# A two-layer trunk on one core: seven block products at the end of the first stage, and a setup for the S5 mixer spread over other engines and another stage

## The chip, the cores and the metric

The kernel runs on one core of one Trainium2 chip. The metric is the device time of one execution in microseconds (us). Engines are named as in the profile: PE is TensorE's matmul side and PEld its weight load, DVE is VectorE, ACT is ScalarE, POOL is GpSimd, SP is SyncE. A name with a q at its end (ACTq, POOLq, SPq) is that engine's instruction that issues a DMA.

## The reference

Two layers over x of 512 positions by 1024 columns, all in float32. The first has an SSD (Mamba-2) mixer, the second an S5 mixer, and each has a SwiGLU block before and after it.

```python
D_MODEL, SEQ, DEPTH, FFN_DIM = 1024, 512, 2, 2816

def swiglu(h, w_in, w_out):
    gate, up = jnp.split(h @ w_in, 2, axis=-1)
    return (jax.nn.silu(gate) * up) @ w_out

def reference(x, ...):
    for i in range(DEPTH):
        x = x + 0.5 * swiglu(rmsnorm(x, ffn1_norm[i]), ffn1_w_in[i], ffn1_w_out[i])
        h = rmsnorm(x, mix_norm[i])
        x = x + (ssd_mixer(h, ...) if i % 3 == 0 else s5_mixer(h, ...))
        x = x + 0.5 * swiglu(rmsnorm(x, ffn2_norm[i]), ffn2_w_in[i], ffn2_w_out[i])
    return rmsnorm(x, final_norm)

def s5_mixer(h, ...):                      # 64 groups of 16 columns, 64 complex states each
    lam_bar = jnp.exp(lam * step)
    b_bar = ((lam_bar - 1.0) / lam)[..., None] * lax.complex(b_re, b_im)
    # states[t] = lam_bar * states[t-1] + b_bar @ u[t];  y[t] = Re(c @ states[t]) + d * u[t]
    # then gelu, a product with glu_w, and value * sigmoid(gate)
```

What depends on the S5 weights alone (powers of lam_bar, the operators built from b, c and d, and tables of cosines and sines of its angles) can be made before the S5 mixer's input is there.

## The kernel before

Six stages follow each other: `f1_0` (SwiGLU), `ssd`, `f2_0` (SwiGLU), `f1_1` (SwiGLU), `s5`, `f2_1` (SwiGLU). In the profiled execution they end at about 390, 807, 1148, 1496, 1630 and 1981 us.

The residual stream is kept transposed as eight tiles `xT[d]` of 128 columns by 512 positions. Every float32 operand of a matmul is split into a high and a low part, and a product takes three matmuls (high by high, low by high, high by low). For weights, ACT casts the high part `whi` from the loaded `wst`, and DVE subtracts to get `wlo`. For a stage's normed input the parts are `H[d]` and `L[d]` (`hH`, `hL` in the profile).

**A SwiGLU stage** (`ffn`) has 22 pairs: a pair is one block of 128 gate columns and the block of 128 up columns beside it. They come in three parts, `PARTS` = (0, 8), (8, 15), (15, 22). After each part come eight out-projection columns d = 0..7: the part's activations `ah`, `al` times one block of out-weights, added to `xT[d]` by DVE.

- A *plain* pair is 2 x 8 x 3 = 48 matmuls with 512 columns (lines 374 to 376).
- A pair *as seven products* uses a block scheme over 2 x 2 blocks with seven block products instead of eight: 7 x 4 x 3 = 84 matmuls with 256 columns (line 445). It needs sums of input blocks, the forms (`forms`: tiles `hx`, `h1`, each again high by ACT and low by DVE), sums of weight blocks (`wx`, `wst`, made partly by DMAs that accumulate, issued on POOL), and more DVE work behind each product.

In `f1_0` all 22 pairs are plain. In `f2_0` the first three (`PLAIN`) are plain and 19 are as seven products; in `f1_1` and `f2_1` all 22.

**Order.** The tile framework's scheduler sets the order of instructions on each engine by its own estimate. Within `manual_schedule(engines=MAN)` (`f2_0` and all later stages) PE keeps the order in which the code is written; the other engines are ordered by the scheduler except for instructions that are pinned. In `f1_0` the scheduler orders PE too. Whatever the origin, the order on each engine is fixed when the program is built: an instruction that waits holds up all behind it on that engine.

**Work for S5 in other stages.** A list `fill` of closures is passed to `ffn`, and `pop()` runs the next one after each pair and each column: 22 + 24 = 46 pops, of which the columns are pops 8 to 15, 23 to 30 and 38 to 45. In `f1_0` this list holds the S5 setup: `lam` (lam_bar, its powers `PR`, `PI`, the angles), `ops(i)` for i = 0..15 (operators of four groups each: six DVE products and sums of 512 or 576 elements, line 1064, tiles `p_Ht`, `p_G`, `p_t`), `ops_pe(i)` (transposes and small products on PE; ACT copies the result into `p_ks`, DVE adds the diagonal with d by 64 small instructions in all, line 1349, and eight DMAs on ACT's queue write it out, line 1353), and `tables(i)` for i = 0..7 (`p_cs`, `p_tb`, from the angle powers `p_UC`, `p_US` by doubling, for eight of the 64 groups each, written to `d_t` by POOL).

**The step from `f2_0` to `f1_1`.** Behind the last columns of `f2_0` DVE adds `xT[6]` and `xT[7]` (line 683), makes `hL` of column 6 and 7 (lines 272, 286), the forms `hx` (lines 303, 307), the low parts of the first pair's weights (line 410) and the norm `nw_*` (lines 147 to 156), while PE goes on with products of the first pair of `f1_1` as far as their operands are there.

## Time and profile before

| what | value |
|---|---|
| median of 3 runs | 1981.26 us (1981.21 to 1982.32) |
| profiled execution: its own time | 1983.18 us |
| profiled execution: span | 1981.4 us, so 1.8 us lie outside the span |
| PE busy in the span | 1964.9 us (99%) |
| DVE busy | 1524.8 us (77%) |
| ACT busy | 944.7 us (48%) |
| POOL busy | 237.1 us (12%) |
| granted TensorE clock | 0.999 |

The profile is one execution. A busy share is an average over the six stages, and the engines' loads differ between the stages. PE takes its matmuls strictly in order, so whether a stage is bound by PE or by what feeds it is seen from PE's idle time in that stage and from what ended it.

### The profile page before, as it was taken

What the parts mean: (1) busy time and instruction counts of PE and PEld (TensorE: products, weight loads), DVE (VectorE), ACT (ScalarE), POOL (GpSimd) and SP (SyncE); (2) the same over time, 40 slices, a digit from 0 to 9 for tenths busy, and PEclk for the clock granted to TensorE, in tenths of its full rate; (3) what the DMA queues carried; (4) which work ended last, traced back from release to release, by engine and by line L of the source; (5) the groups of instructions that cost most, each with busy time, mean ns of one, the idle gap of its engine ahead of it and who ended that gap; (6) DMA issues with size and microseconds to landing.
All of it is one profiled execution on the core that took longest, in us unless ns stands there. A gap on an engine that the chain in (4) does not pass through costs nothing.

```text
span 1981.4 us, 32556 instructions
## 1 busy us (share of the span) xinstructions
PE 1964.9 (99%) x12669; PEld 1735.2 (88%) x12669; DVE 1524.8 (77%) x2630; ACT 944.7 (48%) x1472; POOL 237.1 (12%) x261
## 2 busy tenths in 40 slices
PE   9999999999999999999999999999999999999998
PEld 7888888888888888898989899898988789999897
DVE  6898986888888678875858887585868668667685
ACT  5322233565565355552525555352557446435363
POOL 1000000012111110111202111120201112111110
PEclk9999999999999999999999999999999999999999
DMA  7444564544333422684858767585998348667572
GB/s 191 107 138 146 155 194 128 138 126 133 114 105 113 116 88 76 134 185 107 182 122 176 187 142 172 115 177 121 185 265 284 89 105 174 160 136 167 122 158 86
DMA packets 503994, 288.28 MB, mean 145 GB/s; under 512 B 47808, under 2 KB 489312, under 8 KB 503840
## 3 DMA queue, kind: packets, MB, share of 16 engines
q1 hardware_dynamic: 408384, 217.02, 38.7%
q0 software_dynamic: 73728, 55.28, 16.9%
q10 hardware_dynamic: 21728, 13.91, 2.5%
q8 instruction: 99, 1.62, 0.3%
q14 instruction: 55, 0.45, 0.1%
HBM read 264.60 MB, written 21.04 MB: 144 GB/s over the span
## 4 chain that ended last, share of the span: by engine, by line
PE 93%; DVE 3%; DMA 2%; ACT 1%; issue 1%; ACTq 0%; SPq 0%; DVEq 0%
PE mm L445 31%; PE mm L374 18%; PE mm L375 18%; PE mm L376 18%; DMA wst<-in_s_glu_w_dram 1%; PE aux L959 1%; PE aux L901 1%; PE aux L1564 1%; PE aux L951 0%; DMA xt<-in_x_dram 0%; PE aux L852 0%; PE aux L376 0%; PE aux L375 0%; PE aux L374 0%; DMA opP<-d_P 0%
## 5 line engine op out<-in xcount | busy, mean ns | idle before, releaser
L365 ACT CAST whi<-wst 128x1024 fp32r<-128x1024 f32 (+2 forms) x220 | 216.9, 991 | 412.7 <-PE mm L375 275.4
L374 PE MATMUL mm<-hH,whi 128*128 128x512 f32 x776 | 306.3, 395 | 0.0
L375 PE MATMUL mm<-hL,whi 128*128 128x512 f32 x776 | 302.4, 390 | 0.0
L376 PE MATMUL mm<-hH,wlo 128*128 128x512 f32 x776 | 302.4, 390 | 0.0
L445 PE MATMUL mm<-hx,whi 128*128 128x256 f32 x1512 | 280.8, 283 | 0.0
L367 DVE TENSOR_TENSOR wlo<-wst,whi 128x1024 fp32r<-128x1024 f32 (+2 forms) x220 | 253.7, 1155 | 29.2 <-ACT whi L365 27.2
L374 PE MATMUL mm<-ah,whi 128*128 128x512 f32 x648 | 252.7, 391 | 0.0
L375 PE MATMUL mm<-al,whi 128*128 128x512 f32 x648 | 252.5, 390 | 0.0
L376 PE MATMUL mm<-ah,wlo 128*128 128x512 f32 x648 | 251.9, 390 | 0.0
L445 PEld LDWEIGHTS mm<-hx,whi 128*128 128x128 f32 x1512 | 236.4, 192 | 0.7
L410 DVE TENSOR_TENSOR wlo<-wst,whi 128x1024 fp32r<-128x1024 f32 x126 | 154.3, 1224 | 91.8 <-ACT whi L407 88.7
L445 PE MATMUL mm<-hx,wlo 128*128 128x256 f32 x756 | 214.1, 283 | 0.2 <-DVE wlo L410 0.2
L445 PE MATMUL mm<-hL,whi 128*128 128x256 f32 x672 | 190.3, 283 | 0.5 <-DVE hL L272 0.3
L445 PE MATMUL mm<-hH,wlo 128*128 128x256 f32 x672 | 190.6, 284 | 0.2
L445 PE MATMUL mm<-hH,whi 128*128 128x256 f32 x672 | 190.3, 283 | 0.0
L376 PEld LDWEIGHTS mm<-hH,wlo 128*128 128x128 f32 x776 | 145.6, 188 | 30.6
L374 PEld LDWEIGHTS mm<-hH,whi 128*128 128x128 f32 x776 | 145.7, 188 | 30.4 <-issue 0.7
L375 PEld LDWEIGHTS mm<-hL,whi 128*128 128x128 f32 x776 | 145.8, 188 | 29.5 <-issue 0.2
L407 ACT CAST whi<-wst 128x1024 fp32r<-128x1024 f32 x126 | 131.6, 1045 | 37.3 <-PE mm L375 29.6
L445 PEld LDWEIGHTS mm<-hx,wlo 128*128 128x128 f32 x756 | 145.1, 192 | 0.4 <-DVE wlo L410 0.4
L376 PEld LDWEIGHTS mm<-ah,wlo 128*128 128x128 f32 x648 | 121.6, 188 | 25.3
L375 PEld LDWEIGHTS mm<-al,whi 128*128 128x128 f32 x648 | 121.7, 188 | 24.8 <-issue 0.4
(499 smaller groups left out, 3936.3 us busy)
## 6 DMA issues: line engine op xcount, KB each, us to landing
wst<-in_ffn_w_in_dram SPq DMA_DIRECT2D x175, 512.0 KB, 4.4
wst<-in_ffn_w_out_dram SPq DMA_DIRECT2D x56, 448.0 KB, 4.2
wst<-in_ssd_in_proj_dram SPq DMA_DIRECT2D x48, 512.0 KB, 3.9
wst<-in_ffn_w_out_dram SPq DMA_DIRECT2D x39, 512.0 KB, 4.1
wx<-in_ffn_w_in_dram SPq DMA_DIRECT2D x63, 256.0 KB, 3.2
wx<-in_ffn_w_in_dram POOLq DMA_DIRECT2D x63, 256.0 KB, 6.9
...
```

What stands on the lines that cost most here:

```text
L365: S.copy(hi, st)
L367: V.tensor_tensor(lo, st, hi.bitcast(F32), op=OP.subtract)
L374: PE.matmul(ps, hi[:, k], H[k], start=first and k == 0, stop=False)
L375: PE.matmul(ps, hi[:, k], L[k], start=False, stop=False)
L376: PE.matmul(ps, lo[:, k], H[k], start=False, stop=last and k == n - 1)
L407: self.pin(S.copy(hi, st))
L410: self.pin(V.tensor_tensor(lo[:, c], st[:, c], hi[:, c].bitcast(F32), op=OP.subtract))
L445: PE.matmul(ps, w_[:, j], b_, start=nm not in self.open, stop=False, skip_group_check=True)
L901: PE.matmul(pst[c], st["bt"][:, c * 128:(c + 1) * 128], st["wx"][:, c], start=True, stop=True)
L959: PE.matmul(py[e][hh * 64:(hh + 1) * 64, s], st["dtx"][:, c, k0:k0 + 64], M[:, hh, s], start=True, stop=True)
L1564: PE.matmul(py[i, h][e * 64:e * 64 + 64, g * 128:g * 128 + 128], l[:, h * 4 + g], out_ops(i + e, h)[:, g, w:w + 128], start=first and g == ...
```

## The change

1. **`f1_0`'s last part as seven products.** Pairs 15 to 21 of `f1_0` become pairs as seven products, and PE's order is the written one from pair 15 on. The forms for them are made at the out-projection columns d = 1..4 of the second part: the normed columns are rebuilt on DVE as H + L (`split_only`), since the input columns have been changed by then. `tail` frees the S5 setup's buffers for them. The out-weights of d > 2 are issued behind the last cast of the forms.
2. **The S5 setup in `f1_0` in 23 pops instead of 45.** Of the six products and sums of each `ops(i)`, two products go to GpSimd (`G.tensor_tensor`, 32 in all). The diagonal of `p_ks` takes two DVE instructions per batch instead of eight. The 64 DMAs that write `p_ks` are issued by POOL instead of ACT.
3. **The tables go to `f2_0`.** Angles and tables are made for 32 columns on 128 partitions (half of the groups on each half of the partitions), so there are four tables instead of eight; they are spread over 18 pops, pinned in place at the columns d = 0..5 of each of the three parts: the angles at the first part, two tables at the second, two at the third. ACT issues the DMAs that write them.
4. In the `s5` stage two copies on ACT swap which of them carries the factor -1.

```diff
-        def forms(self, j, fp, hp):
+        def forms(self, j, fp, hp, split_only=False):
 
...
 
             def split(dst, s, src):
-                S.copy(dst[:, 0, s], src)
-                V.tensor_tensor(dst[:, 1, s], src, dst[:, 0, s].bitcast(F32), op=OP.subtract)
+                self.cast = S.copy(dst[:, 0, s], src)
+                return V.tensor_tensor(dst[:, 1, s], src, dst[:, 0, s].bitcast(F32), op=OP.subtract)
 
...
+            b = work.tile([128, T], F32, tag="sq", name="tb")
+            if split_only:
+                he, le, ho, lo_ = [t_[i].bitcast(F32) for i in (e, o) for t_ in (self.H, self.L)]
+                V.tensor_tensor(a[:, lo], he[:, lo], le[:, lo], op=OP.add)
+                V.tensor_tensor(a[:, hi], a[:, lo], he[:, hi], op=OP.subtract)
+                V.tensor_tensor(a[:, hi], a[:, hi], le[:, hi], op=OP.subtract)
+                V.scalar_tensor_tensor(b[:, lo], ho[:, hi], -1.0, a[:, hi], op0=OP.mult, op1=OP.subtract)
+                V.tensor_tensor(b[:, lo], b[:, lo], lo_[:, hi], op=OP.subtract)
+            else:
+                S.activation(a[:, lo], xT[e][:, lo], AF.Copy, scale=ge)
+                V.scalar_tensor_tensor(a[:, hi], xT[e][:, hi], ne, a[:, lo], op0=OP.mult, op1=OP.add)
+                V.scalar_tensor_tensor(b[:, lo], xT[o][:, hi], no, a[:, hi], op0=OP.mult, op1=OP.subtract)
             split(self.w1, s, a[:, hi])
-            V.scalar_tensor_tensor(b[:, lo], xT[o][:, hi], no, a[:, hi], op0=OP.mult, op1=OP.subtract)
             V.scalar_tensor_tensor(b[:, hi], b[:, lo], -1.0, a[:, lo], op0=OP.mult, op1=OP.subtract)
             z = hx[0].tile([128, 2, T], F32R, name="hx", bufs=6)
             split(z, slice(0, T), b)
-            V.scalar_tensor_tensor(a[:, lo], xT[o][:, lo], no, b[:, lo], op0=OP.mult, op1=OP.subtract)
-            split(self.w, s, a[:, lo])
+            if split_only:
+                V.scalar_tensor_tensor(a[:, lo], ho[:, lo], -1.0, b[:, lo], op0=OP.mult, op1=OP.subtract)
+                V.tensor_tensor(a[:, lo], a[:, lo], lo_[:, lo], op=OP.subtract)
+            else:
+                V.scalar_tensor_tensor(a[:, lo], xT[o][:, lo], no, b[:, lo], op0=OP.mult, op1=OP.subtract)
+            formed = split(self.w, s, a[:, lo])
...
+            return formed
...
-    def seven_first(pr, w_in, f, fp):
+    def seven_first(pr, w_in, f, fp, u=None, after=None):
+        u = u or Seven(pr, w_in, f, fp)
         u.split_g()()
-        u.sum2()
-        u.sum4()
+        with tc.issue_after(after.ins) if after else ExitStack():
+            u.sum2()
+            u.sum4()
         u.pin = tc.keep_in_program_order
...
-    def ffn(pr, w_in, w_out, nxt, fill=(), ready=(), done=(), gates=(), hp=None):
+    def ffn(pr, w_in, w_out, nxt, fill=(), ready=(), done=(), gates=(), hp=None, tail=None):
...
+        if tail:
+            plain = PARTS[-1][0]
...
+                if tail and a == plain:
+                    seven = True
+                    by_hand.enter_context(tc.manual_schedule(engines=MAN))
...
-                        proj(pd, load_w(w_out[a * 128:b * 128, d * 128:(d + 1) * 128], b - a), AH, AL)
+                        with tc.issue_after(pr.cast.ins) if tail and b == plain and d > 2 else ExitStack():
+                            w_d = load_w(w_out[a * 128:b * 128, d * 128:(d + 1) * 128], b - a)
+                        proj(pd, w_d, AH, AL)
+                    if tail and b == plain:
+                        if d == 1:
+                            hp = tail()
+                        if d in (1, 2, 3, 4):
+                            formed = pr.forms(d - 1, fp, hp, split_only=True)
+                        if d == 4:
+                            u = Seven(pr, w_in, b, fp)
+                        elif d == KD - 1:
+                            u = seven_first(pr, w_in, b, fp, u, formed)
...
-            t2h = t2.rearrange("p g m c -> p (g m c)")[:, 0:512].rearrange("p (g c q) -> p g c q", g=4, c=16)
             tt(Ht, be(st["ER"]), bb(B1), OP.mult)
-            tt(t2h, be(st["EI"]), bb(B2), OP.mult)
-            tt(Ht, Ht, t2h, OP.add)
-            G9 = pp.tile([128, 4, 9, 16], F32, tag="p_wg", name="p_G9", bufs=2)
+            G.tensor_tensor(t1, be(st["EI"]), bb(B2), op=OP.mult)
+            G.tensor_tensor(t2, bm(st["PI"], 9), bc(C2, 9), op=OP.mult)
+            tt(Ht, Ht, t1, OP.add)
             tt(G9, bm(st["PR"], 9), bc(C1, 9), OP.mult)
-            tt(t2, bm(st["PI"], 9), bc(C2, 9), OP.mult)
             tt(G9, G9, t2, OP.add)
...
-            for g in range(8):
-                kg = ks[:, g, 0:16]
-                V.scalar_tensor_tensor(kg, ident[0:16, 0:16], s5["dT"][:, 4 * i + g:4 * i + g + 1], kg,
-                                       op0=OP.mult, op1=OP.add)
+            dg = pp.tile([16, 8, 16], F32, name="p_dg", bufs=1)
+            tt(dg, ident[0:16, None, 0:16].to_broadcast([16, 8, 16]),
+               s5["dT"][:, 4 * i:4 * i + 8][:, :, None].to_broadcast([16, 8, 16]), OP.mult)
+            tt(ks[:, :, 0:16], ks[:, :, 0:16], dg, OP.add)
             for q in range(8):
-                nc.scalar.dma_start(ov[q, :, 4 * i:4 * i + 8, 128 + 16 * q:256], ks[:, :, 0:128 - 16 * q])
+                G.dma_start(ov[q, :, 4 * i:4 * i + 8, 128 + 16 * q:256], ks[:, :, 0:128 - 16 * q])
...
+    def s5_tables(tp):
...
+        def angles():
+            usq(c, s)
+            usq(c, s)
+            yield
+            usq(c, s)
+            for j in range(6):
+                pin(V.tensor_copy(UC[:, j], c))
+                pin(V.tensor_scalar(US[:, 0, j], s, -1.0, None, op0=OP.mult))
+                pin(V.tensor_copy(US[:, 1, j], s))
+                if j < 5:
+                    usq(c, s)
+                if j < 4:
+                    yield
+            yield
+            for i in range(4):
...
+                cs = tp.tile([128, 2, 8, 64], F32, name="t_cs", bufs=3)
+                tb = tp.tile([128, 2, 8, 32], F32, name="t_tb", bufs=1)
+                for j in range(6):
+                    w = 1 << j
...
+                    o, t_ = cs[:, :, :, w:2 * w], tb[:, :, :, 0:w]
+                    tt(o, a_, bR, OP.mult)
+                    if j == 5:
+                        yield
+                    tt(t_, sw, bI, OP.mult)
+                    tt(o, o, t_, OP.add)
+                    if j == 3:
+                        yield
+                for h in range(2):
+                    for e in range(2):
+                        nc.scalar.dma_start(s5["t"][i + 4 * h][64 * e:64 * e + 64], cs[64 * h:64 * h + 64])
+                yield
...
+                    def tail():
+                        pre_es.close()
+                        hx.append(third.enter_context(tc.tile_pool(name="hx0", bufs=6, reuse_waits="tile")))
+                        return third.enter_context(tc.tile_pool(name="h10", bufs=2, reuse_waits="tile"))
+
+                    ffn(pr, wi[L], wo[L], nxt, fill=pre0, ready=ready, done=done, gates=[first_gate], tail=tail)
...
+                    tabs, fill = s5_tables(tp), [lambda: None] * 46
+                    for n in (*range(8, 14), *range(23, 29), *range(38, 44)):
+                        fill[n] = tabs.pop(0)
+                    ffn(pr, wi[L], wo[L], nxt, fill=fill, hp=hp)
```

How the order of instructions moves, at three places. Names carry the program's buffer numbers.

DVE at the out-projection columns of the second part of `f1_0`, before: `mm_2239` is the product of column d = 2, `mm_2279` of d = 3 (its out-weights are `wlo_2284`), and `wlo_2314` are the low out-weights of d = 4.

```order
L683 SCALAR_TENSOR_TENSOR xT0_85<-mm_2139,xT0_85 128x512
L683 SCALAR_TENSOR_TENSOR xT1_86<-mm_2169,xT1_86 128x512
L367 TENSOR_TENSOR wlo_2284<-wst_2280,whi_2282 128x896
L1064 TENSOR_TENSOR p_Ht_2228<-p_rER_1054,p_B1_1235 128x512
L1064 TENSOR_TENSOR p_G9_2233<-p_PR_856,p_C_1228 128x576
L367 TENSOR_TENSOR wlo_2314<-wst_2310,whi_2312 128x896
L1064 TENSOR_TENSOR p_Ht_2268<-p_rER_1054,p_B1_1235 128x512
L1064 TENSOR_TENSOR p_G9_2273<-p_PR_856,p_C_1228 128x576
L1349 SCALAR_TENSOR_TENSOR p_ks_2207<-ident_76,p_dT_128,p_ks_2207 16x16 x6
L683 SCALAR_TENSOR_TENSOR xT2_87<-mm_2239,xT2_87 128x512
```

The low out-weights of d = 3 and d = 4 stand ahead of the addition of column 2. The same place in the changed program; `mm_2396` is the product of d = 2, `wlo_2447` are the low out-weights of d = 3:

```order
L340 TENSOR_TENSOR ta_2472<-hH_243,hL_245 128x256
L330 TENSOR_TENSOR hx_2434<-tb_2425,hx_2434 128x512
L715 SCALAR_TENSOR_TENSOR xT2_87<-mm_2396,xT2_87 128x512
L330 TENSOR_TENSOR hx_2377<-ta_2424,hx_2377 128x256
L341 TENSOR_TENSOR ta_2472<-ta_2472,hH_243 128x256
L381 TENSOR_TENSOR wlo_2447<-wst_2443,whi_2445 128x896
L340 TENSOR_TENSOR ta_2518<-hH_267,hL_269 128x256
L342 TENSOR_TENSOR ta_2472<-ta_2472,hL_245 128x256
L341 TENSOR_TENSOR ta_2518<-ta_2518,hH_267 128x256
```

They now stand behind the addition of column 2. Further down on DVE the low out-weights of d = 4 (`wlo_2495`) follow after the last of eighteen forms instructions that begin with `ta_2518` above:

```order
L350 SCALAR_TENSOR_TENSOR tb_2519<-tb_2519,ta_2518 128x256
L355 TENSOR_TENSOR ta_2472<-ta_2472,hL_262 128x256
L330 TENSOR_TENSOR hx_2482<-tb_2473,hx_2482 128x512
L354 SCALAR_TENSOR_TENSOR ta_2518<-hH_274,tb_2519 128x256
L330 TENSOR_TENSOR hx_2471<-ta_2472,hx_2471 128x256
L355 TENSOR_TENSOR ta_2518<-ta_2518,hL_276 128x256
L381 TENSOR_TENSOR wlo_2495<-wst_2491,whi_2493 128x896
L715 SCALAR_TENSOR_TENSOR xT3_88<-mm_2442,xT3_88 128x512
```

So between the low weights of d = 3 and those of d = 4 stand 18 instructions of 256 or 512 elements, where there were two. On PE, in the changed program, the columns follow each other in these rows:

```order
L390 MATMUL mm_2396<-ah_2267,wlo_2401 128x512
L388 MATMUL mm_2442<-ah_1664,whi_2445 128x512
L389 MATMUL mm_2442<-al_1666,whi_2445 128x512
L390 MATMUL mm_2442<-ah_1664,wlo_2447 128x512
L388 MATMUL mm_2442<-ah_1784,whi_2445 128x512
```

The third matmul of column 3 (`mm_2442`) reads `wlo_2447`; nothing else stands between the columns. The second place is DVE at the last columns of `f2_0`, before: the operands of `f1_1`'s first pair behind `xT[7]`.

```order
L683 SCALAR_TENSOR_TENSOR xT6_91<-mm_11074,xT6_91 128x512
L410 TENSOR_TENSOR wlo_11155<-wst_11102,whi_11154 128x1024
L435 TENSOR_TENSOR wst_11106<-wst_11106,wx_11104 128x4x128
L303 TENSOR_TENSOR hx_11063<-tb_11059,hx_11063 128x512
L307 TENSOR_TENSOR hx_11064<-tc_11060,hx_11064 128x256
L270 SCALAR_TENSOR_TENSOR ta_11113<-xT6_91,ngs_117,ta_11113 128x256
L215 TENSOR_TENSOR acc_10879<-acc_10879,sq_11118 128x512
L683 SCALAR_TENSOR_TENSOR xT7_92<-mm_11121,xT7_92 128x512
L272 TENSOR_TENSOR hL_11112<-ta_11113,hH_11111 128x512
```

After, the table instructions (line 1383, tiles `t_cs` and `t_tb`) stand among them; two excerpts, the first around `xT[7]`:

```order
L1383 TENSOR_TENSOR t_cs_11204<-t_cs_11204,t_UC_7787 128x16x32
L1383 TENSOR_TENSOR t_tb_11205<-t_cs_11204,t_US_7788 128x512
L215 TENSOR_TENSOR acc_11202<-acc_11202,sq_11493 128x512
L715 SCALAR_TENSOR_TENSOR xT7_92<-mm_11496,xT7_92 128x512
L303 TENSOR_TENSOR hx_11432<-tb_11428,hx_11432 128x512
L270 SCALAR_TENSOR_TENSOR ta_11488<-xT6_91,ngs_117,ta_11488 128x256
L307 TENSOR_TENSOR hx_11433<-tc_11429,hx_11433 128x256
L1383 TENSOR_TENSOR t_cs_11204<-t_cs_11204,t_tb_11205 128x16x32
L288 SCALAR_TENSOR_TENSOR tb_11541<-xT7_92,ngs_117,ta_11488 128x256
L272 TENSOR_TENSOR hL_11487<-ta_11488,hH_11486 128x512
```

The second is around the norm's first row:

```order
L424 TENSOR_TENSOR wl4_11619<-wst_11481,wh4_11618 128x512
L307 TENSOR_TENSOR hx_11433<-tc_11542,hx_11433 128x256
L424 TENSOR_TENSOR wlo_11538<-wx_11479,whi_11537 128x512
L1383 TENSOR_TENSOR t_cs_11337<-t_cs_11337,t_tb_11338 128x16x16
L147 TENSOR_SCALAR nw_h_11672<-aux_11634 128x4
L1383 TENSOR_TENSOR t_cs_11337<-t_cs_11337,t_UC_7787 128x16x32
L1383 TENSOR_TENSOR t_tb_11338<-t_cs_11337,t_US_7788 128x512
L148 TENSOR_SCALAR nw_y_11674<-nw_h_11672 128x4
L1383 TENSOR_TENSOR t_cs_11337<-t_cs_11337,t_tb_11338 128x16x32
```

All of the first of the two tables (`t_cs_11204`) stands ahead of `hL` of column 6 (`hL_11487`), and the second (`t_cs_11337`) ends among the norm's instructions. The third place is POOL in `f1_0`, which before has there only the DMAs that write the tables; after:

```order
L1315 TENSOR_TENSOR p_t1_1898<-p_rEI_938,p_B2_1047 128x512
L1316 TENSOR_TENSOR p_t2_1899<-p_PI_719,p_C_819 128x576
L1315 TENSOR_TENSOR p_t1_1981<-p_rEI_938,p_B2_1047 128x512
L1355 DMA d_P_119<-p_ks_1882 16x8x128
L1355 DMA d_P_119<-p_ks_1882 16x8x112
```

The products of `ops` and the DMAs of `p_ks` share POOL's one order.

More of the change, by code (lines that the diff above doesn't have):

```diff
@@ L317, in combine @@
                 split_c()()
-        def forms(self, j, fp, hp):
+        def forms(self, j, fp, hp, split_only=False):
             lo, hi = slice(0, 256), slice(256, 512)
             e, o = 2 * j, 2 * j + 1
-            ge, ne, no = col(self.gain[0], self.gain[1] + e), self.ng[:, e:e + 1], self.ng[:, o:o + 1]
+            if not split_only:
+                ge, ne, no = col(self.gain[0], self.gain[1] + e), self.ng[:, e:e + 1], self.ng[:, o:o + 1]
             for nm, d, s in (("11", e, lo), ("21", o, lo), ("22", o, hi)):
@@ L559, in seven_in @@
         pop()
-    def seven_first(pr, w_in, f, fp):
-        u = Seven(pr, w_in, f, fp)
+    def seven_first(pr, w_in, f, fp, u=None, after=None):
+        u = u or Seven(pr, w_in, f, fp)
         u.split_g()()
-        u.sum2()
-        u.sum4()
+        with tc.issue_after(after.ins) if after else ExitStack():
+            u.sum2()
+            u.sum4()
         u.pin = tc.keep_in_program_order
@@ L688, in ffn @@
                 fill.pop(0)()
+            by_hand.close()
         nxt.finish()
@@ L1206, in lam @@
             yield
-            nr, ni, den, c0r, c0i = sm("nr"), sm("ni"), sm("den"), sm("c0r"), sm("c0i")
+            den = sm("den")
+            nr, ni, c0r, c0i = [pp.tile([128, 64], F32, tag="p_" + t_, name="p_" + nm, bufs=1)
+                                for nm, t_ in (("nr", "ea"), ("ni", "en"), ("c0r", "er"), ("c0i", "et"))]
             tt(er, em, c, OP.mult)
@@ L1357, in s5_setup, with b @@
         one = lambda: next(gen)
-        fill = [masks, lambda: None, rows] + [both(one, lambda j=j: load_c(j)) for j in range(3)] + [one] * 3
-        fill += [both(lambda i=i: c_cols(i), lambda i=i: load_b(2 * i), lambda i=i: load_b(2 * i + 1)) for i in range(4)]
-        tabs = [lambda i=i: tables(i) for i in range(8)]
+        def b(*js):
+            return lambda: [load_b(j) for j in js]
         zero = [lambda q=q: zeros(q) for q in range(1, 8)]
-        steps = [both(lambda i=i: i and i % 2 == 0 and ops_pe(i - 2), lambda i=i: ops(i)) for i in range(16)] + [lambda: ops_pe(14)]
@@ L1363, in s5_setup @@
-        fill += [both(tabs[0], swap_b)] + tabs[1:4] + [both(lambda: None, zero[0])] + steps[:2] + zero[1:2]
-        for n, f in enumerate(steps[2:]):
-            fill.append(f)
-            if n % 2 and zero[2 + n // 2:3 + n // 2]:
-                fill.append(zero[2 + n // 2])
-            if n % 4 == 3:
-                fill.append(tabs[4 + n // 4])
-        return fill + tabs[4 + (len(steps) - 2) // 4:]
+        steps = [both(lambda i=i: i and i % 2 == 0 and ops_pe(i - 2), lambda i=i: ops(i)) for i in range(16)]
@@ new lines, in s5_setup @@
+        fill = [masks, both(rows, one, lambda: load_c(0), lambda: load_c(1)), both(one, lambda: load_c(2), b(0, 1)),
+                both(one, b(2, 3)), both(one, lambda: c_cols(0), b(4, 5)), both(one, lambda: c_cols(1), b(6, 7)),
+                both(one, lambda: c_cols(2), swap_b), both(steps.pop(0), lambda: c_cols(3), zero.pop(0))]
+        while steps:
+            f = steps.pop(0)
+            if len(fill) == 16:
+                f = both(f, steps.pop(0))
+            fill.append(both(f, zero.pop(0)) if zero and len(fill) % 2 else f)
```

106 lines of the change are left out of this document (53 added, 53 removed).

## The prediction

> **What bounds the kernel now.** I read the page's busy shares first, then PE's busy time by stretches with the list of what PE waited for, then single rows of DVE and PE where the change puts work. The page's first rows, busy time per engine and then the chain that ended last:
>
> ```profile
> PE 1964.9 (99%) x12669; PEld 1735.2 (88%) x12669; DVE 1524.8 (77%) x2630; ACT 944.7 (48%) x1472; POOL 237.1 (12%) x261
> PE 93%; DVE 3%; DMA 2%; ACT 1%; issue 1%; ACTq 0%; SPq 0%; DVEq 0%
> ```
>
> PE is idle for 16.5 us of the whole span. Which stretches these are not in is seen in the busy times by stretch (start and end; its length, then busy us of PE, PEld, DVE, ACT, POOL, each with its number of instructions; clock; DMA share):
>
> ```profile
> core 0: us, PE busy (x) PEld busy (x) DVE busy (x) ACT busy (x) POOL busy (x), PEclk, DMA share, GB/s
> 16.00:390.00 374.00, 374.00 (x1853) 305.61 (x1855) 315.82 (x750) 130.47 (x189) 4.48 (x9) 1.00 0.54 146
> 886.00:930.00 44.00, 44.00 (x201) 36.67 (x200) 21.81 (x29) 9.52 (x10) 2.54 (x2) 1.00 0.48 114
> 1000.00:1039.00 39.00, 39.00 (x180) 32.49 (x179) 20.79 (x29) 8.94 (x10) 2.54 (x2) 1.00 0.51 119
> 1140.00:1158.00 18.00, 17.72 (x174) 16.01 (x173) 17.26 (x37) 9.44 (x17) 1.27 (x1) 1.00 0.41 92
> 1158.00:1229.00 71.00, 71.00 (x593) 71.00 (x592) 58.33 (x87) 42.76 (x65) 16.53 (x13) 1.00 0.82 173
> ```
>
> In `f1_0` PE is busy for all of 374 us. So taking work off DVE or ACT there gives nothing by itself: the change can only gain where PE's own work gets less, and it loses wherever PE's next operand comes late. The row 1140 to 1158, the step from `f2_0` to `f1_1`, is the other kind: DVE is busy 17.26 of 18 us. What PE waited for from 1100 to 1170 us:
>
> ```profile
> PE mm L445 <- DVE hL L272: 0.3, 1, 0.3
> ```
>
> PE and DVE both run full there, and PE waited for DVE already.
>
> **Term 1, fewer matmul columns: -5.6 us.** Rows of PE in single matmuls (a column's stretch, no idle between), then of the chain of work for 256-column products:
>
> ```profile
> 1114.53 0.40 PE L374 MATMUL mm<-ah,whi 128*128 128x512 f32 x1
> 1138.34 0.39 PE L374 MATMUL mm<-ah,whi 128*128 128x512 f32 x1
> 1158.43 70.55 PE mm L445 x588
> ```
>
> Between the first two are 35 groups of three, so 23.81 / 105 = 0.2268 us per matmul of 512 columns; a plain pair takes 48 x 0.2268 = 10.88 us. The third row is seven pairs as seven products (588 = 7 x 84): 10.08 us each. Seven pairs save 7 x 0.80 = 5.6 us, in a stretch that is all PE. This is the whole gain that the change can have.
>
> **Term 2, the forms at the columns of `f1_0`'s second part: +4.6 us.** Busy time, then mean ns: DVE's low out-weights and column additions and ACT's high out-weights in `f1_0`, and single DVE rows of 256 and 512 elements (each next one starts 0.34 or 0.60 us later):
>
> ```profile
> L367 DVE TENSOR_TENSOR wlo<-wst,whi 128x896 fp32r<-128x896 f32 x16 | 17.3, 1081 | 0.2
> L683 DVE SCALAR_TENSOR_TENSOR xT<-mm,xT 128x512 f32<-128x512 f32 x24 | 16.3, 685 | 10.2 <-PE mm L376 10.1
> L365 ACT CAST whi<-wst 128x896 fp32r<-128x896 f32 x16 | 14.9, 940 | 31.4 <-PE mm L375 22.0 <-DMA d_P<-p_ks 5.3 <-issue 3.9
> 1127.44 0.68 DVE L303 TENSOR_TENSOR hx<-tb,hx 128x512 fp32r<-128x512 f32 x1
> 1128.04 0.42 DVE L307 TENSOR_TENSOR hx<-tc,hx 128x256 fp32r<-128x256 f32 x1
> ```
>
> By the new order DVE's low weights of d = 3 stand behind the addition of column 2, which waits for PE to end d = 2. Call that end 0. Addition 0.60, two of 256 elements 0.68, then the low weights: there at 1.28 + 1.08 = 2.36. PE has two matmuls of d = 3 ahead, 0.45 us: it loses 1.9 and ends d = 3 at 21 x 0.2268 + 1.9 = 6.7. DVE meanwhile goes on at 2.3 with the 18 forms instructions, 17 x 0.34 + 0.60 = 6.4, and has the low weights of d = 4 at 8.7 + 1.08 = 9.8; ACT's casts for these forms wait on DVE and give way for `whi` of d = 4 at about 8.6, which is earlier. PE wanted them at 6.7 + 0.45: it loses 2.6. From d = 5 on the weights stand ahead of the additions that wait. Ends: 1.9, since the first loss has nothing that could hide it, and 9, if in addition one load of out-weights lands late:
>
> ```profile
> wst<-in_ffn_w_out_dram SPq DMA_DIRECT2D x56, 448.0 KB, 4.2
> ```
>
> I take 4.6: the order is fixed and its durations have rows.
>
> **Term 3, two tables at the last columns of `f2_0`: +9.2 us.** DVE's instructions on `p_cs` in `f1_0`, in all, before (length; DVE busy; POOL's issues):
>
> ```profile
> 16.00:390.00 374.00, 43.66 (x156) 4.30 (x8) 1.00 0.54 146
> ```
>
> A table takes 43.66 / 8 = 5.46 us of DVE; the new ones have the same shape (16 x 32 = 512 elements in the last step). Two take 10.9 us. DVE at that place, with the idle time ahead of a row in brackets:
>
> ```profile
> 1138.54 0.69 DVE L683 SCALAR_TENSOR_TENSOR xT<-mm,xT 128x512 f32<-128x512 f32 x1 [0.95 <-PE mm L376]
> 1148.75 0.69 DVE L272 TENSOR_TENSOR hL<-ta,hH 128x512 fp32r<-128x512 f32 x1
> 1152.38 0.69 DVE L303 TENSOR_TENSOR hx<-tb,hx 128x512 fp32r<-128x512 f32 x1 [0.41 <-ACT hx L302]
> 1152.99 0.69 DVE L410 TENSOR_TENSOR wl<-wst,wh 128x512 fp32r<-128x512 f32 x1
> 1156.22 0.16 DVE L156 SCALAR_TENSOR_TENSOR nw_y<-nw_a,nw_y 128x4 f32<-128x4 f32 x1
> 1156.91 1.22 DVE L410 TENSOR_TENSOR wlo<-wst,whi 128x1024 fp32r<-128x1024 f32 x1
> ```
>
> And PE's readers of these:
>
> ```profile
> 1149.49 0.39 PE L445 MATMUL mm<-hL,whi 128*128 128x256 f32 x1 [0.28 <-DVE hL L272]
> 1154.51 0.50 PE L445 MATMUL mm<-hx,whi 128*128 128x256 f32 x2
> 1155.20 0.28 PE L445 MATMUL aux<-hH,wl 128*128 128x256 f32 x1
> 1157.84 0.60 PE L191 MATMUL aux<-ident,nw_y 128*128 128x128 f32 x4
> 1158.51 0.28 PE L445 MATMUL mm<-hH,wlo 128*128 128x256 f32 x1
> ```
>
> The only idle time that DVE has from 1118.8 to 1158 are the two bracketed gaps, 0.95 and 0.41. Ahead of `hL` of column 6 stand all of the first table and 0.25 of the second: `hL` comes 5.46 + 0.25 - 0.95 = 4.8 later, and PE, which was waiting for it, loses 4.8. Then, each time the delay of DVE against PE's delay plus its slack in the rows: the last `hx`, 6.6 against 4.8 + 1.4, loses 0.4; `wl`, 7.4 against 5.2 + 1.5, loses 0.7; the norm's last row, now 10.9 - 1.36 = 9.5 late, against 5.9 + 1.4, loses 2.2; the second pair's low weights, 9.5 late, against 8.1 + 0.4, lose 1.1. Together 9.2. Ends: 4.8 (`hL` alone) and 10.9. I take 9.2. DVE has room again after 1158 (58.33 of 71), but PE's lost time is not given back.
>
> **The other parts, 0.** The angles at the first columns and two tables at the second have room: 21.81 of 44 busy plus 64 + 18 small instructions of some 0.22 us, 18 us, and 20.79 of 39 plus 10.9; out-weights stand two columns ahead there (0 to +2). The denser S5 setup in `f1_0` trades with what leaves it. Rows of the two products that go to POOL, of the diagonal, and of `wlo` beside a POOL instruction (in `ssd`) and on the average:
>
> ```profile
> L1064 DVE TENSOR_TENSOR p_t<-p_PI,p_C 128x576 f32<-128x576 f32 x16 | 11.9, 746 | 0.1
> L1064 DVE TENSOR_TENSOR p_t<-p_rEI,p_B 128x512 f32<-128x512 f32 x16 | 11.0, 687 | 0.3
> L1349 DVE SCALAR_TENSOR_TENSOR p_ks<-ident,p_dT,p_ks 16x16 f32<-16x16 f32 x64 | 10.4, 217 | 0.0
> 458.40 1.12 POOL L923 TENSOR_SCALAR_AFFINE_SELECT dec<-dec 128x1024 f32<-128x1024 f32 x1
> 458.63 1.98 DVE L367 TENSOR_TENSOR wlo<-wst,whi 128x1024 fp32r<-128x1024 f32 x1
> L367 DVE TENSOR_TENSOR wlo<-wst,whi 128x1024 fp32r<-128x1024 f32 x52 | 63.3, 1220 | 4.4 <-ACT whi L365 4.2
> ```
>
> DVE is freed of 22.9 us of products and some 7 of the diagonal. But beside a POOL instruction `wlo` took 1.98 instead of 1.22 us: 0.76 more, and 32 such POOL products would give 24 back. So the move frees nothing on DVE by this row, and costs nothing: with the tables gone, DVE's load per pair up to pair 14 stays where it was, and PE was never short there. Ends: 0, as PE has no idle time to win, and +8, a third of the 24, if it falls on low weights that PE wants at once. The 64 DMA issues leave ACT and go to POOL, which is busy 4.5 of 374 us.
>
> [...] No row here shows a GpSimd product.
>
> **Sum.** -5.6 + 4.6 + 9.2 = +8.2 us. The profiled execution (1983.18 us: span 1981.4 and 1.8 outside) would go to 1991.4. It lies 1.9 above the median, so against the median of 1981.26 I predict 1989.5.
>
> **Rivals.**
> - *The tables fit at the last columns, and the change is faster.* Place: DVE ahead of `hL` of column 6. For it: in 1100 to 1170 PE waited 0.3 us only, and small instructions could run in gaps that rows do not show. Against it: busy 17.26 of 18. If `hL` comes less than 1.7 us late and term 2 is 1.9, time falls: -5.6 + 1.9 gives 1977.6, and 1975.7 if term 2 vanished too.
> - *Both losses at their lower ends:* -5.6 + 1.9 + 4.8 = +1.1, 1982.4, no change. For it: later waits may be covered by the first. Against: each waits on a later instruction of the same late DVE.
> - *POOL's products hold up DVE in `f1_0`, and PE with it:* a third of the 24 us on top of the sum, 1997.5; it decides from one delay in ten on, which would be 2 us. For it the 1.98 us row, against it that DVE has idle time there (315.82 of 374).
>
> **How the numbers follow.** Forecast with both losses, 1985 to 1995: 0.55. First rival 0.18, second 0.15, third 0.12. The range 1976 to 1999 reaches from the first rival's times to the third's and leaves out about 0.1. About 0.2% (4 us) is what a measurement of this kernel can tell from no change; faster by more 0.18, within 0.17, slower 0.65.
>
> **What would show it.** Term 1: 588 products of 256 columns in `f1_0` at 10.08 us a pair. Term 2: PE idle at two out-projection columns of the second part, released by DVE's `wlo`. Term 3: PE idle at `hL`, at the transposes of `nw_y` and at `wlo` where `f1_1` begins, some 9 us in all, with DVE busy on `t_cs`. POOL: rows of its products, and DVE products beside them longer than their mean. The prediction is wrong if PE shows no idle time at these places, or if idle time shows elsewhere, at the first pair of seven products in `f1_0` or where `f1_0` gives way to `ssd`.

## The result, and the profile after

The changed kernel is slower: 1995.45 us against 1982.24 us of before on the same chips, a ratio of 1.0066 with the 95% interval 1.0055 to 1.0077, that is 13.2 us (10.9 to 15.3). The forecast was 8.2 us more, 1989.5 against 1981.26; 1995.45 lies at the upper edge of its main band (1985 to 1995). The traces are single executions: that of the changed kernel (1994.67 us, span 1992.9, 11.5 over the span of before) is the fastest of its six, so the account below is made for 11.5 us, while that of the run with the forms behind the out-weights is the slowest of its eleven (1989.86 us, the median is 1986.33).

Busy time per engine of the changed kernel, then the shares of the chain that ended last:

```profile
PE 1966.3 (99%) x12921; PEld 1747.2 (88%) x12921; DVE 1546.0 (78%) x2566; ACT 968.3 (49%) x1519; POOL 337.8 (17%) x363
PE 89%; DVE 7%; issue 1%; ACT 1%; DMA 1%; POOL 0%; DVEq 0%; ACTq 0%; POOLq 0%
```

PE is now idle for 26.6 us instead of 16.5, and DVE's share of the chain has gone from 3% to 7%. What PE waited for in `f1_0` (16 to 400 us), where before there was no wait at all, then at the step from `f2_0` to `f1_1` (1130 to 1175 us):

```profile
PE mm L390 <- DVE wlo L381: 2.6, 2, 2.0
PE mm L388 <- ACT whi L379: 2.4, 2, 1.3
PE aux L1342 <- DVE p_G L1097: 2.2, 1, 2.2
```

```profile
PE mm L459 <- ACT hH L271: 3.0, 1, 3.0
PE mm L459 <- DVE wlo L424: 0.9, 1, 0.9
PE mm L459 <- DVE hL L272: 0.7, 1, 0.7
PE aux L191 <- DVE nw_y L156: 0.4, 1, 0.4
```

These 12.2 us of idle time do not say what the places cost, since PE also ran at half clock behind two of them (a granted clock of 0.50 in each us from 178 to 180 and from 1157 to 1163; rows in the part on the prediction). Delay is the better measure: when PE ends the last out-projection matmul of a part, against before, read from the rows of these matmuls (line 374 to 376 before, 388 to 390 after). In us, for all kernels of this study:

| kernel | `f1_0` part 2 | `f1_0` part 3 | `f2_0` part 2 | `f2_0` part 3 | `f1_1` part 1 | `f2_1` part 1 |
|---|---|---|---|---|---|---|
| changed kernel | +15.6 | +5.2 | +4.2 | +5.7 | +13.5 | +11.4 |
| two tables left out | +14.3 | +4.0 | +3.0 | +4.4 | +4.4 | +2.7 |
| two tables at the pairs, written by ACT | +13.4 | +3.1 | +2.2 | +22.7 | +22.7 | +21.0 |
| the same, written by POOL | +13.7 | +3.4 | +2.4 | +7.5 | +7.5 | +9.2 |
| last part of `f1_0` plain | +5.5 | +0.5 | -0.4 | +0.1 | +9.2 | +9.4 |
| S5 products on DVE | +10.4 | +0.1 | -0.6 | +0.6 | +9.4 | +9.0 |
| forms behind the out-weights | +5.2 | -5.1 | -6.1 | -5.1 | +4.3 | +6.5 |
| combined | +4.9 | -5.5 | -6.3 | -1.3 | -1.3 | -0.4 |
| forms behind, two tables left out | +4.8 | -5.5 | -6.6 | -5.6 | -5.6 | -6.8 |
| combined, scheduler places tables | +5.1 | -5.2 | +0.8 | +0.7 | +0.8 | +0.3 |
| combined, tables two pops earlier | +5.2 | -5.1 | -6.2 | +0.5 | +0.5 | -0.4 |
| combined, even pieces | +5.6 | -4.7 | -5.6 | -3.4 | -1.3 | -1.6 |
| even pieces, products on GpSimd | +5.4 | -4.9 | -6.0 | -3.8 | +0.4 | -0.3 |

The first column holds about 5 us that are no loss: S5 work of PE that stood in part 3 before is done earlier. From the second column on the work done is alike. The changed kernel loses 5.2 us in `f1_0` where its matmuls are 5.6 us shorter, wins 1 in `ssd`, loses 1.5 in `f2_0`'s last pairs, 7.8 at the step to `f1_1`, and wins 2.1 in `s5`. The 2.1 in `s5` cannot be put down to the change: with the same code there, the traces of this study go from 2.1 won to 2.2 lost, and in the two that lose most (forms behind the out-weights; tables at the pairs written by POOL) PE runs at half clock for some 3.4 us of it. Why `ssd` is about 1 us shorter in nearly all of these kernels is open.

PE and DVE at that step, in the rows that answer to those of before (the bracket is idle time):

```profile
1157.83 0.58 PE L459 MATMUL mm<-hH,whi 128*128 128x256 f32 x1 [3.02 <-ACT hH L271]
1170.03 0.65 PE L191 MATMUL aux<-ident,nw_y 128*128 128x128 f32 x4 [0.44 <-DVE nw_y L156]
1171.77 0.39 PE L459 MATMUL mm<-hH,wlo 128*128 128x256 f32 x1 [0.85 <-DVE wlo L424]
```

```profile
1157.39 0.67 DVE L1383 TENSOR_TENSOR t_cs<-t_cs,t_tb 128x512 f32<-128x512 f32 x1
1158.39 0.67 DVE L272 TENSOR_TENSOR hL<-ta,hH 128x512 fp32r<-128x512 f32 x1
1168.03 0.69 DVE L1383 TENSOR_TENSOR t_cs<-t_cs,t_tb 128x512 f32<-128x512 f32 x1
1169.81 0.16 DVE L156 SCALAR_TENSOR_TENSOR nw_y<-nw_a,nw_y 128x4 f32<-128x4 f32 x1
1170.50 1.22 DVE L424 TENSOR_TENSOR wlo<-wst,whi 128x1024 fp32r<-128x1024 f32 x1
```

`hL` of column 6 ran at 1148.75 before and at 1158.39 now; 5.7 of these 9.6 us were there already, so the tables put it off by 3.9. The second pair's `wlo` went from 1156.91 to 1170.50, 7.9 us beyond those 5.7. DVE is busy without a gap between the two.

### The profile page after: what moved, and what is told of

The parts are those of the page before. It is cut to its first block, busy times and chain, and to the rows that moved or that the text cites. A ratio compares the mean times of both kernels' runs of the same rounds, so it can differ in the third digit from the quotient of the medians.

```text
span 1992.9 us, 33200 instructions
## 1 busy us (share of the span) xinstructions
PE 1966.3 (99%) x12921; PEld 1747.2 (88%) x12921; DVE 1546.0 (78%) x2566; ACT 968.3 (49%) x1519; POOL 337.8 (17%) x363
## 4 chain that ended last, share of the span: by engine, by line
PE 89%; DVE 7%; issue 1%; ACT 1%; DMA 1%; POOL 0%; DVEq 0%; ACTq 0%; POOLq 0%
PE mm L459 34%; PE mm L388 16%; PE mm L390 16%; PE mm L389 16%; DVE wlo L381 1%; PE aux L992 1%; DVE wlo L424 1%; PE aux L1634 1%; PE aux L934 1%; DVE p_Ht L1097 0%; PE aux L984 0%; DVE xT L715 0%; PE aux L885 0%; PE aux L390 0%; PE aux L389 0%
## 5 line engine op out<-in xcount | busy, mean ns | idle before, releaser
L459 PE MATMUL mm<-hx,whi 128*128 128x256 f32 x1680 | 312.0, 283 | 0.4 <-ACT gt L473 0.4
L459 PEld LDWEIGHTS mm<-hx,whi 128*128 128x128 f32 x1680 | 262.6, 192 | 1.4 <-ACT gt L473 0.6
L388 PE MATMUL mm<-hH,whi 128*128 128x512 f32 x664 | 263.5, 397 | 0.0
L390 PE MATMUL mm<-hH,wlo 128*128 128x512 f32 x664 | 259.6, 391 | 0.0
L389 PE MATMUL mm<-hL,whi 128*128 128x512 f32 x664 | 259.6, 391 | 0.0
L459 PE MATMUL mm<-hx,wlo 128*128 128x256 f32 x840 | 237.9, 283 | 0.2 <-DVE wlo L424 0.2
L406 POOL DMA_DIRECT2D wx<-in_ffn_w_in_dram x70 | 91.1, 1316 | 563.6 <-DMA wx<-in_ffn_w_in_dram 188.5
L405 POOL DMA_DIRECT2D wst<-in_ffn_w_in_dram x70 | 90.0, 1286 | 384.9 <-DMA wst<-in_ffn_w_in_dram 176.9
L388 PEld LDWEIGHTS mm<-hH,whi 128*128 128x128 f32 x664 | 125.0, 188 | 25.6 <-issue 0.5
L389 PEld LDWEIGHTS mm<-hL,whi 128*128 128x128 f32 x664 | 125.2, 188 | 25.4 <-issue 0.3
```

Of the source, the lines that this page charges most:

```text
L388: PE.matmul(ps, hi[:, k], H[k], start=first and k == 0, stop=False)
L389: PE.matmul(ps, hi[:, k], L[k], start=False, stop=False)
L390: PE.matmul(ps, lo[:, k], H[k], start=False, stop=last and k == n - 1)
L405: G.dma_start(self.half(self.wu, 0), uo, accum_op=OP.add)
L406: G.dma_start(self.x[:, 0], ue, accum_op=OP.add)
L459: PE.matmul(ps, w_[:, j], b_, start=nm not in self.open, stop=False, skip_group_check=True)
```

## The experiments

**Leaving out the two last tables.** Short diff: the loop over the tables does no DVE work for the third and fourth, and writes the first two in their place.

```diff
+                if i > 1:
+                    cs = made[i - 2]
+                    yield
+                    yield
...
+                    continue
```

> Leaves out the third batch of tables: the two tables at the last columns of f2_0 are not computed, the first two are written in their place. Theory (DVE instructions of the tables delay the operands of f1_1's first pair): the step from f2_0 to f1_1 is again as before, so some 7.8 us less than the changed kernel, 1987 to 1988, that is 5 to 6 us over before; PE's waits at hH, hL, nw_y and wlo there vanish, and so does the half clock behind them. Rival (what is late there is ACT's hH or the norm for another reason, or the clock falls by itself): 1995, no change against the changed kernel.

1986.75 us, ratio 1.0022 (1.0012 to 1.0031). The step to `f1_1` keeps the delay that it enters with (+4.4 and +4.4), the granted clock is 1.00 from 1150 to 1165 us, and PE's only wait from 1100 to 1175 us is the one that the kernel before has, too:

```profile
PE mm L459 <- DVE hL L272: 0.3, 1, 0.3
```

The tables' DVE work at these columns is the cause.

**The same tables at the pairs ahead of the columns.**

```diff
-                    for n in (*range(8, 14), *range(23, 29), *range(38, 44)):
+                    for n in (*range(8, 14), *range(23, 29), *range(31, 37)):
```

> The same two tables, moved from the columns d = 0..5 of f2_0's third part to the pairs 15 to 20 ahead of them. Theory (the place counts, not the amount): DVE is busy about 58 of 71 us over seven pairs, and 10.9 more just fit, so the 7.8 us at the step to f1_1 go, and 0 to 3 us come back in the pairs: 1987 to 1991. Rival (the amount counts, DVE has no room for it anywhere in f2_0's third part): the loss only moves, 1994 to 1997.

2005.16 us, ratio 1.0112 (1.0096 to 1.0127): worse than both theories. The step to `f1_1` is free, but `f2_0`'s last pairs lose 20.5 us. PE's waits from 1045 to 1180 us, then rows of ACT, and PE behind them:

```profile
PE mm L459 <- ACT gt L475: 11.6, 2, 5.9
```

```profile
1080.49 4.96 ACTq L1435 DMA_DIRECT2D d_t<-t_cs  x4
1085.49 0.37 ACT L475 COPY gt<-mm 128x256 f32<-128x256 f32 x1 [6.92 <-issue]
```

```profile
1085.91 0.80 PE L459 MATMUL mm<-hx,whi 128*128 128x256 f32 x2 [5.87 <-ACT gt L475]
```

```profile
1085.00:1092.00 7.00, 6.08 (x35) 6.09 (x36) 3.31 (x5) 2.63 (x4) 0.40 (x1) 0.64 0.83 212
```

Most of it is neither DVE's load nor the amount: ACT waits 1.9 us for the table's last DVE instruction, then takes 4.96 us to issue the four DMAs that write it; the copy of PE's result (`gt`, line 475) stands behind them, and PE cannot go on. The second table does the same at 1125.67 us, with issues of 3.81 us. In the last row, a stretch of 7 us behind the wait, the granted clock is 0.64 (the number before DMA share and GB/s), so PE lost time again after the wait. I had not looked at ACT as an issuer of DMAs at all here.

**The same with POOL as the issuer.**

```diff
-                        nc.scalar.dma_start(s5["t"][i + 4 * h][64 * e:64 * e + 64], cs[64 * h:64 * h + 64])
+                        G.dma_start(s5["t"][i + 4 * h][64 * e:64 * e + 64], cs[64 * h:64 * h + 64])
```

> As the run with the third batch of tables at pairs 15 to 20 (2005 us), but the 16 DMAs that write the tables are issued by POOL instead of ACT. Theory (there ACT's four issues in a row, 4.96 us, held up the copies of PE's results, PE waited 11.6 us for them and ran at half clock twice for 6.8 us): that goes, and the step to f1_1 is free as well: 1986 to 1990. Rival (the pinned table instructions hold up DVE's work in the pairs): 2000 to 2005.

1991.85 us, ratio 1.0042 (1.0030 to 1.0055), 13.3 us less than with ACT. In the traces the loss in the pairs falls from 20.5 to 5.1 us, so ACT's waiting and issuing was the larger part. The other 5.1 us stay: the rival has a part, too. DVE is busy nearly throughout there (in the combined kernel below, 1040 to 1110 us):

```profile
1040.00:1110.00 70.00, 68.00 (x530) 64.95 (x529) 67.49 (x123) 36.01 (x56) 19.93 (x20) 1.00 0.87 188
```

**The last part of `f1_0` plain again**, without forms: `ffn` is called without `tail`.

```diff
-                    ffn(pr, wi[L], wo[L], nxt, fill=pre0, ready=ready, done=done, gates=[first_gate], tail=tail)
-                    hx.clear()
+                    ffn(pr, wi[L], wo[L], nxt, fill=pre0, ready=ready, done=done, gates=[first_gate])
+                    pre_es.close()
```

> The last seven pairs of f1_0 are plain again and no forms are made there; S5 setup and tables as in the changed kernel. Theory (the forms cost about what the seven products gain): +5.6 for the matmuls, -4.7 for the waits at the columns of the second part: 1995 to 1997. Rival (the waits in f1_0 come from the denser S5 setup alone, the forms are free): +5.6, 2001.

1991.24 us, ratio 1.0038 (1.0025 to 1.0050): 4.2 us faster than the changed kernel, which neither had. `f1_0` has no wait of PE left, also none for `p_G`, though the S5 setup is as dense and its products are on GpSimd. So the last part as seven products cost more than the waits at the columns that I had counted; the loss ahead of them, near 120 and 176 us, goes away with them.

**The S5 products back on DVE.**

```diff
-            G.tensor_tensor(t1, be(st["EI"]), bb(B2), op=OP.mult)
-            G.tensor_tensor(t2, bm(st["PI"], 9), bc(C2, 9), op=OP.mult)
+            V.tensor_tensor(t1, be(st["EI"]), bb(B2), op=OP.mult)
+            V.tensor_tensor(t2, bm(st["PI"], 9), bc(C2, 9), op=OP.mult)
```

> The 32 products of the S5 setup that were given to GpSimd are back on DVE. Theory (beside GpSimd's products DVE's two-input instructions are held up by about as much as DVE was freed of): DVE's load stays, but without the long instructions the wait for p_G near 176 us, the half clock behind it and the wait near 120 us shrink: 1990 to 1994. Rival (GpSimd does relieve DVE, which is over-full with the products): 22.9 us more on DVE in 120 us that have none to spare, and PE waits 5 to 15 us longer: 2000 to 2010.

1992.26 us, ratio 1.0043 (1.0030 to 1.0055), 3.2 us less than the changed kernel: as expected. DVE's busy time from 16 to 236 us, where both do the whole S5 setup, in the changed kernel and then here (third pair of numbers):

```profile
16.00:236.00 220.00, 216.69 (x1098) 175.49 (x1096) 198.51 (x358) 80.51 (x122) 77.20 (x90) 0.99 0.63 157
```

```profile
16.00:236.00 220.00, 219.72 (x1118) 178.51 (x1118) 191.41 (x392) 83.20 (x129) 32.94 (x63) 1.00 0.65 162
```

DVE is busy 7.1 us *less* with the 32 products (22.8 us) on it. Groups of the changed kernel, DVE's `wlo` and one of its products in that stretch and POOL's two kinds of products, then the first two with the products on DVE:

```profile
L381 DVE TENSOR_TENSOR wlo<-wst,whi 128x1024 fp32r<-128x1024 f32 x36 | 49.1, 1370 | 0.7 <-ACT whi L379 0.5
L1097 DVE TENSOR_TENSOR p_Ht<-p_rER,p_B 128x512 f32<-128x512 f32 x11 | 10.9, 998 | 0.0
L1315 POOL TENSOR_TENSOR p_t<-p_rEI,p_B 128x512 f32<-128x512 f32 x16 | 23.9, 1493 | 24.1 <-DVE p_X L1097 12.5 <-DVE p_Ht L1097 9.1 <-DMA p_B<-p_B 2.4
L1316 POOL TENSOR_TENSOR p_t<-p_PI,p_C 128x576 f32<-128x576 f32 x16 | 23.8, 1490 | 78.6 <-DVE p_PI L1283 62.5 <-DVE p_G L1097 11.7 <-DVE p_X L1097 4.4
```

```profile
L381 DVE TENSOR_TENSOR wlo<-wst,whi 128x1024 fp32r<-128x1024 f32 x36 | 43.7, 1216 | 0.6 <-ACT whi L379 0.3
L1097 DVE TENSOR_TENSOR p_Ht<-p_rER,p_B 128x512 f32<-128x512 f32 x11 | 7.4, 682 | 0.0
```

With the products on GpSimd `wlo` takes 1370 ns instead of 1216 and a product on DVE 998 instead of 682; those on POOL take 1.49 us on the average, where one with DVE idle beside it took 1.07 (at 116.04 us). DVE also stands idle for GpSimd's results, 5.0 us in the changed kernel up to 236 us:

```profile
DVE p_Ht L1097 <- POOL p_t L1315: 3.1, 2, 2.7
DVE p_G L1097 <- POOL p_t L1316: 1.9, 2, 1.3
```

**The forms behind the out-weights.** At the columns of `f1_0`'s second part each column's out-weights are loaded and split two columns ahead, and the forms are queued behind them on ACT and DVE.

```diff
...
-                        with tc.issue_after(pr.cast.ins) if tail and b == plain and d > 2 else ExitStack():
-                            w_d = load_w(w_out[a * 128:b * 128, d * 128:(d + 1) * 128], b - a)
-                        proj(pd, w_d, AH, AL)
+                        for e in range(d, min(d + 3, KD) if tail and b == plain else d + 1):
+                            if e not in early:
+                                early[e] = load_w(w_out[a * 128:b * 128, e * 128:(e + 1) * 128], b - a)
...
+                            with tc.issue_after(last_split[0].ins), tc.issue_after(last_split[1].ins):
+                                formed = pr.forms(d - 1, fp, hp, split_only=True)
...
```

> Only the order at the columns of f1_0's second part is changed: each column's out-weights are loaded and split two columns ahead, and the forms stand behind them on ACT and DVE. Theory (the forms cost because low and high out-weights stand behind them): the waits for wlo and whi at these columns, 3.9 us and some 5 us in PE's time, go: 1990 to 1991.5. Rival (the forms need the time wherever they stand): they are late for the first seven-product pair instead, 1994 to 1996.

1986.33 us, ratio 1.0015 (1.0006 to 1.0024): 9.1 us less than the changed kernel, twice what I expected, and still with the products on GpSimd. PE is busy in all of the stage:

```profile
16.00:400.00 384.00, 384.00 (x2181) 326.61 (x2180) 317.34 (x558) 166.07 (x249) 99.73 (x111) 1.00 0.63 151
```

At the columns 4.9 us are won (the delay grows by 3.4 over them in the changed kernel and falls by 1.5 here), and 5.5 ahead of them (part 2's columns begin 12.2 us late in the changed kernel and 6.7 here). The second share is the surprise. The code makes the forms at the columns d = 1..4, but in the changed kernel the scheduler had put the sums of the first two of the four sets far ahead. The first of them in the changed kernel and then here:

```profile
42.30 0.74 DVE L340 TENSOR_TENSOR ta<-hH,hL 128x256 f32<-128x256 f32 x2
```

```profile
239.14 0.42 DVE L340 TENSOR_TENSOR ta<-hH,hL 128x256 f32<-128x256 f32 x1
```

These are 16 DVE instructions from 42.3 to 58.7 us; the high and low parts of the same forms are made only from 239 us on. So DVE's room early in `f1_0` went to sums that nobody wanted before 236 us, and the S5 setup behind them was late: its first product (`p_Ht`) ran at 103.25 us in the changed kernel and at 93.89 here. DVE's waits for GpSimd's products up to 236 us fall from 5.0 to 2.6 us with it.

**The three repairs together**: forms behind the out-weights, products on DVE, two tables at the pairs and written by POOL.

> The three repairs together: forms behind the out-weights, S5 products on DVE, third batch of tables at pairs 15 to 20 with POOL's DMAs. If each loss is what the theory says and they add up, the seven products' 5.6 us are left, with about 1 to 2 us won in the s5 stage: 1975 to 1978, faster than before. If a loss only moves (rival), between 1980 and 1990.

1981.88 us, ratio 0.9998 (0.9989 to 1.0007): no different from before, and 3.9 us over what I expected. `f1_0` and `ssd` keep 6.3 us; `f2_0`'s last pairs take 5.0 of them back, as with the tables there alone, and the 1 to 2 us that I expected from `s5` do not come (0.9 lost).

**Forms behind the out-weights, two tables left out.**

> Forms behind the out-weights, and the third batch of tables left out (two tables are not computed, the first two are written in their place); S5 products on GpSimd as in the changed kernel. What the change would be worth without its two losses. Theory: the run with the forms behind (1986.3) less the step to f1_1 (9 us): 1976 to 1978.5, that is the 5.6 us of the seven products and little else. Rival (the two losses overlap, or the gain is not there): 1980 to 1983.

1978.68 us, ratio 0.9984 (0.9975 to 0.9993), faster than before by 3.2 us (1.4 to 5.0). Between the two profiled executions it is 6.7, but this kernel's lies 2.2 us under its median and that of before over its own. So a gain is there once both losses are away, in the traces of about the size of term 1; but this kernel does half of the tables only.

**Three attempts to place the tables at no cost.** Unpinned tables, which the scheduler then puts into `f2_0`'s first part:

```diff
-        pin = tc.keep_in_program_order
+        pin = lambda i: i
```

> The combined kernel with the table instructions not pinned: the scheduler places all angles and tables in f2_0's first part, just ahead of and among its pairs. DVE has 85 of 123 us busy there and gets some 40 more. Theory (DVE's room in a stretch decides): it is full there, PE waits 2 to 8 us in f2_0's first part, 1979 to 1984. Rival (only pinned instructions at the wrong place hurt, the scheduler's order does not): 1976 to 1978.

1983.43 us, ratio 1.0005 (0.9996 to 1.0014), at the upper end: PE waits 4.1 us for `wlo` in `f2_0`'s first part and some 7 us are lost there. Two pops earlier (`range(29, 35)`):

> The combined kernel with the third batch of tables two pops earlier: at the columns d = 6, 7 of f2_0's second part and the pairs 15 to 18. DVE is busy about 21 of 39 us in those columns, so a third of the batch finds room, and the last pairs before the columns have none of it: the 5 us that the batch cost in the pairs falls to 2 to 4: 1978 to 1981. Rival (at the columns' end DVE prepares the next pair, as it does at the step to f1_1): 1982 to 1985.

1983.51 us, ratio 1.0006 (0.9997 to 1.0015): the rival holds, the wait (2.7 for `wlo`) is at the first pair behind the columns. And even pieces over the pairs and one column:

```diff
-                    if j == 5:
+                    if j > 3:
                         yield
...
-                    if j == 3:
+                    if j == 2:
                         yield
...
-                    for n in (*range(8, 14), *range(23, 29), *range(31, 37)):
-                        fill[n] = tabs.pop(0)
+                    for n in (*range(8, 14), 23, 24, 25, 26, 27, 28, *range(31, 39)):
+                        fill[n] = both(tabs.pop(0), tabs.pop(0)) if n in (23, 25) else tabs.pop(0)
```

> The combined kernel with each table cut into four pieces of 1.2 to 1.7 us instead of three of 1.2 to 2.6, and the third batch at the pairs 15 to 21 and the first column behind them. Theory (a piece ahead of the next pair's weights holds DVE up by its length, and what is over the slack of about a microsecond costs): the 5.0 us in these pairs fall to 1 to 3: 1978 to 1980.5, faster than before. Rival (the sum of the work counts, not its pieces): 1982, as the combined kernel.

1981.81 us, ratio 0.9996 (0.9987 to 1.0005). The pairs lose 2.2 instead of 5.0, as expected, but the last pieces put off `hH` at the step to `f1_1`, which loses 2.1. With the products on GpSimd:

> The same with the S5 products on GpSimd as in the changed kernel. Theory (with the forms behind the out-weights no PE wait is left in f1_0 either way): within 1 us of the run with the products on DVE. Rival (GpSimd's products cost PE time by holding up DVE): 3 us more.

1983.25 us, ratio 1.0004 (0.9996 to 1.0013), 1.4 us more, of which some 0.35 lie outside the span, so the two theories are not told apart by the times. By the traces `f1_0` has no wait in either, and loses nothing to GpSimd (-6.0 and -5.6 behind `ssd`); the difference is at the step to `f1_1`, which has nothing on GpSimd but more idle time, 2.2 us against 1.6, and half clock behind it:

```profile
1147.53 0.38 PE L461 MATMUL mm<-hH,whi 128*128 128x256 f32 x1 [2.21 <-ACT hH L271]
```

```profile
1150.00:1155.00 5.00, 5.00 (x90) 4.85 (x88) 3.40 (x7) 2.08 (x5) 0.36 (x1) 0.68 0.61 99
```

No version with all tables beats the kernel before; the combined one and the even pieces are equal to it within their intervals.

## Why the prediction was right, and where it was not

- **Term 1, the seven products (-5.6).** Right. All 588 products of 256 columns are there, and with the waits away `f1_0` ends 5.1 us earlier (forms behind the out-weights) or 5.5 (the same with two tables left out).
- **Term 2, the forms at the columns (+4.6).** Right in place and size: 4.9 us, by waits for `wlo` of 2.0 and 0.6 and for `whi` of 1.3 (the forecast had `whi` of d = 4 at 8.6 and PE ready for it at 6.7, so this wait was in its numbers, though its signs name `wlo` alone). Putting the out-weights ahead takes them away.
- **Term 3, two tables at the step to `f1_1` (+9.2).** Right in mechanism: `hL`, the norm and the second pair's `wlo` come late one after the other. It cost 7.8 us in the changed kernel's trace, and 9.1, 8.7 and 9.4 in three others that leave that place as it is. PE's first wait there was for `hH`, made by ACT from a tile that DVE had late.
- **The other parts, 0.** This is the step that failed, by 7 us: the S5 setup in `f1_0` costs 5.5 us ahead of part 2's columns, and 1.5 are lost in `f2_0`. PE's 2.2 us for `p_G` at 176 us and 1.05 for `whi` at 120 us are idle time at places that the forecast did not name. I took DVE's load per pair as unchanged and weighed GpSimd's products alone (the third rival, 8 us at most). What was missing is that a part of the forms was made there too, at 42 us already, in the same scarce room. Forms early and products on GpSimd are needed both: without the forms (1991.24) or with the products on DVE (1992.26) nearly all of this part goes, and with the forms later it goes with the products still on GpSimd. The other 1.5 us are in `f2_0`'s last pairs, most of it at the first pairs behind the second columns. There ACT issues the second table's four DMAs, and `gt`, for which PE waited 0.4 us, stands behind them:

```profile
1042.85 2.97 ACTq L1435 DMA_DIRECT2D d_t<-t_cs  x4
1046.18 0.37 ACT L473 COPY gt<-mm 128x256 f32<-128x256 f32 x1 [6.69 <-DVE wlo L424]
```

In the seven traces where ACT writes the tables and two of them are made at these columns, 0.5 to 1.2 us are lost up to the second of these pairs. In four where POOL writes them (tables at the pairs written by POOL, combined, and both with even pieces) nothing is lost there, and the first of these four differs from its neighbour with ACT in the issuer alone. So the issues on ACT cost time here, too; the forecast counted DVE's room at these columns and not ACT's.

- **GpSimd's products.** Forecast: DVE is freed of 22.9 us and loses about 24. Measured: DVE is busier by 7.1 us, so it lost 29.9, and it waited for GpSimd's results on top. What the forecast set at about zero is a loss, and it reached PE only where DVE had no room. That `wlo` took 1370 ns instead of 1216 and a product on DVE 998 instead of 682 is measured; why DVE's instructions take longer beside GpSimd's, the traces do not show.
- **What the sum left out.** PE's clock. Behind the 2.20 us wait near 176 us the granted clock fell (from 178 to 180 us matmuls of 512 columns start 0.43 us apart, where ahead of the wait it was 0.23), and behind the waits at the step to `f1_1` as well:

```profile
176.00:181.00 5.00, 4.31 (x26) 3.29 (x27) 4.90 (x5) 1.66 (x2) 4.99 (x8) 0.66 0.93 173
1155.00:1160.00 5.00, 1.47 (x5) 1.18 (x6) 4.97 (x11) 2.71 (x4) 1.28 (x1) 0.67 0.29 55
```

At the first place the delay grew by 4.6 us; 0.8 of it is S5 work of PE that is done earlier there, so some 3.8 us were lost for 2.2 us of idle time. At the second the slow clock added nothing that shows, because DVE was late for PE to the end of the step anyway: the second pair's `wlo` is 7.9 us late by DVE alone.

That 8.2 came as near to 11.5 as it did is in part luck. The other parts cost 7.0 us that had been set at zero and terms 1 and 2 came out 0.8 worse; 3.1 us won in `ssd` and `s5`, which nobody had forecast, and 1.4 us less in term 3 hid more than half of that.
